# Moving sums and lo parts to VectorE, pooling the activations' sums in two, and loading the embedding at once in a fused encoder layer

## The chip, the cores and the metric

The kernel runs on one core of a Trainium2 chip. The metric is the device time of one execution in microseconds (us); lower is better. Engines are named as the profile has them: PE is TensorE's matmul and PEld its weight load, DVE is VectorE, ACT is ScalarE, POOL is GpSimd, SP is the engine that issues most DMAs.

## The reference

One layer of an encoder trunk, for a prompt of 1024 tokens and a sample of 64 (1088 columns here), in float32. In short:

```
xn = rmsnorm(x, norm_mix);  parts = xn @ w_in          # three mixers A, B, C
x  = x + concat(ya, yb, yc) @ w_out                     # output projection, 1536 -> 1024
h  = rmsnorm(x, norm_ffn)
g  = causal_conv3(h @ w_gate)                           # 1024 -> 3072
x  = x + (gelu(g) * (h @ w_up)) @ w_down                # gated MLP
x  = x + sigmoid(rmsnorm(x, norm_ple) @ ple_w_gate) * (p @ ple_w_proj)   # embedding p, 256 wide
y  = rmsnorm(x, norm_final)
```

The states of the mixers and convolutions are outputs too; the change doesn't touch them.

## The kernel before

Activations lie with features on the partitions and tokens along the free dimension, in three chunks of 384, 384 and 320 columns (`CH`). Float32 accuracy comes from split operands: `split` (line 182) writes a hi part by ScalarE (line 184, a copy rounded to fp32r) and a lo part `l = x - h` by a second engine (line 188), and each product is three matmuls, hi x hi, hi x lo and lo x hi (`mm3`, line 156). If no engine is given, the lo part alternates between VectorE and POOL (`alt`, line 180). For weights `unit_load` (line 115) has SP load 512 KB into one of two buffers `wr`, and `unit_split` (line 122) splits it, always with POOL, into a buffer `wh` and a buffer `wl`, of which wpool has three each; `wslots` names the pools in turn.

The program is traced in the order of the text, and a planner then fixes each engine's own order ahead of time, by priority in text order among what it expects to be ready, and places all semaphores. At run time each engine works through its list. A pool of tiles lies on a stack of bytes (or, with side="right", on one from the other end); a pool opened after others are closed takes their bytes.

The stages around the change, in order:
- Output projection in three passes of 512 rows of `w_out` (lines 1023, 1027 and 1086). In the last pass `add_proj` (line 997) loads four weight units first and goes chunk by chunk; `acc` (line 990) adds each result in PSUM to X (`L992`), and squares and their sums are made for the norm (`L208`, `L209`). Lanes are generators that `tick` (line 141) advances every six matmuls: `embedding` (line 1035) loads the nine blocks of p three ahead (`L1041`), turns them with PE (`L1051`) and splits them into pTh and pTl; `norm_rows` (line 1061) scales X in place once a chunk is complete (`L1067`), and after chunk 1 splits the left half of X into qh and ql (`lefts`).
- The embedding's projection (lines 1090 to 1099): two weight units, 24 results, copied to `po` by ScalarE (`L1098`) and written to DRAM.
- The two large products of the MLP run as quads, a Strassen-Winograd scheme: 2 x 2 blocks of weights (128 columns by 512 rows) times 2 x 2 blocks of X (512 rows by 544 columns, `HF`), with seven products instead of eight. The sums of X's blocks (t1, t2, t3, t4 and the plain b22) are made once, in two column parts of 224 and 320 (lines 1116 to 1128), in tiles of the pool rp. For each quad `quad_weights` (line 1140) loads two units, makes s1 to s4 by four POOL operations of 512 elements, and splits seven blocks. `quad` (line 1170) runs the products with three PSUM tiles qa, qb and qd in the order a11, s2, s1, a12, s3, s4, a22; the second four add onto what PSUM holds, so the copy `L1177` and the sums `L1179` to `L1189` have to be done in time.
- 12 pairs of quads, gate and up (lines 1212 to 1237), with the convolution on VectorE (`L1199`, `L1205`, `L1207`) between; results go to DRAM (`hidd`).
- Down projection, six groups (line 1291); norm (`rms`, line 1268); the gate of the embedding and the output (line 1345 on).

The bytes that a partition holds for the pools around the change: xnp (split activations of the last pass) 34,816; ept 26,624 (pTh and pTl 17,408, pt 3 x 1024, po 4 x 1536); wx 24,576; and on the same bytes, after all three are closed, rp with ten tiles of 8704 (87,040) and w2 with s12, s34, dh and dl (12,288).

Of the kernel before, what the change touches and what calls it, by code (L numbers as in the profile page):

```python
# [9 lines left out]
F32 = mybir.dt.float32  # L10
F32R = mybir.dt.float32r
# [16 lines left out]
BLK = [(b // 3, (b % 3) * 128, 128) for b in range(8)] + [(2, 256, 64)]  # L28
# [3 lines left out]
HF = 544  # L32
# [3 lines left out]
def f32(ap):  # L36
    return ap.bitcast(F32)
# [3 lines left out]
def trunk(ctx: ExitStack, tc: tile.TileContext, I, O):  # L41
    nc = tc.nc
    V, A, G, PE, SY = nc.vector, nc.scalar, nc.gpsimd, nc.tensor, nc.sync

    const = ctx.enter_context(tc.tile_pool(name="const", bufs=1))
    wpool = ctx.enter_context(tc.tile_pool(name="wpool", bufs=3))
# [17 lines left out]
    def sm_tile():  # L64
        return smps[0].tile([128, 512], F32, tag="sm", name="sm")
# [44 lines left out]
            pass  # L110


    wslots = {"pools": [wpool], "n": 0}

    def unit_load(ap):

        kt, cols = ap.shape[0] // 128, ap.shape[1]
        raw = wpool.tile([128, kt, cols], F32, tag="wr", name="wr", bufs=2)
        SY.dma_start(raw, ap.rearrange("(k p) n -> p k n", p=128))
        return raw  # L120

    def unit_split(raw):

        pool = wslots["pools"][wslots["n"] % len(wslots["pools"])]
        wslots["n"] += 1
        hi = pool.tile(list(raw.shape), F32R, tag="wh", name="wh")
        lo = pool.tile(list(raw.shape), F32R, tag="wl", name="wl")
        split(hi, lo, raw, G)
        return hi, lo

    def unit(ap):
        return unit_split(unit_load(ap))
# [4 lines left out]
    def lane(gen):  # L137
        lanes.append([gen, 0])
        return gen
# [40 lines left out]
    alt = [V, G]  # L180

    def split(h, l, x, eng=None):

        A.activation(h, x, AF.Copy)  # L184
        if eng is None:
            eng = alt[0]
            alt.reverse()
        eng.tensor_sub(l, x, f32(h))  # L188
# [35 lines left out]
    def tokens(name, b):  # L224
        lead = "a b t d -> (a b t) d" if name == "p" else "b t d -> (b t) d"
        if b < 8:
            return I[name + "_prompt"].rearrange(lead)[b * 128:(b + 1) * 128, :]
        return I[name + "_sample"].rearrange(lead)
# [78 lines left out]
    SY.dma_start(smw[:, :, 32:40], W[:, 4112:4120].rearrange("(k p) n -> p k n", p=128))  # L307
    finish(*[lane(xblock(b)) for b in range(3)])
    wq.append(unit_split(wraw))
    V.tensor_scalar(smh[:, :, 40:64], smw[:, :, 0:24], 0.0, None, op0=OP.mult)  # L310
    split(smh[:, :, 0:40], smh[:, :, 64:104], smw, V)
# [322 lines left out]
    for s in range(2):  # L634
        src = I["ssd_d"]
# [4 lines left out]
    for t, nm in ((dtb, "ssd_dt_bias"), (nea, "ssd_a_log")):  # L640
        src = I[nm]
# [389 lines left out]
    ept = est.enter_context(tc.tile_pool(name="ept", bufs=1, reuse_waits="tile"))  # L1031
# [2 lines left out]

    def embedding():

        pts = {}

        def pload(b):
            pts[b] = ept.tile([128, 256], F32, tag="pt", name="pt", bufs=3)  # L1040
            SY.dma_start(pts[b][:BLK[b][2], :], tokens("p", b))  # L1041

        for b in range(3):
            pload(b)
        yield 4
        for b, (c, off, L) in enumerate(BLK):
            pt = pts.pop(b)
            t0 = CH[c][0] + off
            ps = sm_tile()
            for k in range(2):  # L1050
                PE.transpose(ps[:, k * 128:k * 128 + L], pt[:L, k * 128:(k + 1) * 128], ident[:L, :L])  # L1051
            yield 1
            split(pTt[0][:, :, t0:t0 + L], pTt[1][:, :, t0:t0 + L],
                  ps.rearrange("p (k t) -> p k t", k=4)[:, 0:2, :L], V)
            if b + 3 < 9:
                pload(b + 3)
            yield 1

    lefts = []
# [18 lines left out]
    def spill(c, m):  # L1078
        t0, w = CH[c]
        if m % 2:  # L1080
            SY.dma_start(xspill[:, m - 1:m + 1, t0:t0 + w], XK[m // 4][:, m % 4 - 1:m % 4 + 1, t0:t0 + w])

    emb = lane(embedding())
    wslots["pools"], wslots["n"] = [wpool, wpool, wpool, wx], 0
    normed = []
    add_proj(WO[1024:1536], ys["c"], 4, lambda c: normed.append(lane(norm_rows(c))), spill)
# [19 lines left out]


    rst = ExitStack()
    rp = rst.enter_context(tc.tile_pool(name="rp", bufs=1, reuse_waits="tile"))
    w2 = rst.enter_context(tc.tile_pool(name="w2", bufs=1, reuse_waits="tile"))  # L1110

    def half(name):
        return tuple(rp.tile([128, 4, HF], F32R, name=name + n) for n in "hl")

    b22, t2, t1, t3, t4 = [half(n) for n in ("b22", "t2", "t1", "t3", "t4")]
    for a, n in ((0, 224), (224, 320)):
        s = slice(a, a + n)
        x11, x12 = XK[0][:, :, a:a + n], XK[0][:, :, HF + a:HF + a + n]
        x21, x22 = XK[1][:, :, a:a + n], XK[1][:, :, HF + a:HF + a + n]
        split(b22[0][:, :, s], b22[1][:, :, s], x22)  # L1120
        V.tensor_sub(x22, x22, x12)
        G.tensor_sub(x12, x12, x11)  # L1122
        V.tensor_add(x11, x22, x11)
        split(t2[0][:, :, s], t2[1][:, :, s], x11, V)
        split(t1[0][:, :, s], t1[1][:, :, s], x12, G)
        V.tensor_sub(x21, x21, x11)
        split(t3[0][:, :, s], t3[1][:, :, s], x22, V)
        split(t4[0][:, :, s], t4[1][:, :, s], x21, G)
    b11, b21 = [tuple(t[:, 4 * i:4 * i + 4, :] for t in lefts) for i in range(2)]
    xst2.close()  # L1130

# [8 lines left out]
    def quad_weights(ap):  # L1140

        raw0, raw1 = unit_load(ap[:, 0:128]), unit_load(ap[:, 128:256])
        a11, a12, a21, a22 = raw0[:, 0:4, :], raw0[:, 4:8, :], raw1[:, 0:4, :], raw1[:, 4:8, :]
        al = unit_split(raw0)
        s12 = w2.tile([128, 8, 128], F32, tag="s12", name="s12")
        s1, s2 = s12[:, 0:4, :], s12[:, 4:8, :]
        G.tensor_add(s1, a21, a22)
        G.tensor_sub(s2, s1, a11)
        be = unit_split(s12)
        s34 = w2.tile([128, 8, 128], F32, tag="s34", name="s34")  # L1150
        s3, s4 = s34[:, 0:4, :], s34[:, 4:8, :]
        G.tensor_sub(s3, a11, a21)
        G.tensor_sub(s4, a12, s2)
        ga = unit_split(s34)
        de = tuple(w2.tile([128, 4, 128], F32R, tag=n, name=n) for n in ("dh", "dl"))
        split(de[0], de[1], a22, G)
        part = lambda u, i: tuple(t[:, 4 * i:4 * i + 4, :] for t in u)
        return {"a11": part(al, 0), "a12": part(al, 1), "s1": part(be, 0), "s2": part(be, 1), "s3": part(ga, 0),
                "s4": part(ga, 1), "a22": de}
# [10 lines left out]
    def quad(ap, take11, o12, o21, o22):  # L1170

        w = quad_weights(ap)
        A_, B_, D_ = [qp.tile([128, 2, 512], F32, tag=n, name=n) for n in ("qa", "qb", "qd")]
        pa, pb, pd = [t[:, :, :HI] for t in (A_, B_, D_)]
        o12, o21, o22 = [t.rearrange("p (i n) -> p i n", i=2) for t in (o12, o21, o22)]
        prod(A_, w["a11"], b11, True)
        A.activation(o21, pa, AF.Copy)  # L1177
        prod(B_, w["s2"], t2, True)
        V.tensor_add(o12, o21, pb)  # L1179
        prod(D_, w["s1"], t1, True)  # L1180
        V.tensor_add(o22, o21, pd)
        prod(A_, w["a12"], b21, False)
        take11(pa)
        prod(B_, w["s3"], t3, False)
        V.tensor_add(o22, o22, pb)
        prod(D_, w["s4"], b22, False)
        V.tensor_add(o12, o12, pd)
        prod(B_, w["a22"], t4, False)
        V.tensor_add(o21, o21, pb)  # L1189
# [125 lines left out]
    src = I["norm_final"]  # L1315
# [90 lines left out]
```

## Time and profile before

| | us |
|---|---|
| median of 3 runs (1711.34 to 1718.62) | 1712.57 |
| the profiled execution | 1712.1 |
| its span in the trace | 1710.4 |
| PE busy in the span | 1616.9 (95%) |
| DVE busy | 945.4 (55%) |
| ACT busy | 698.7 (41%) |
| POOL busy | 696.3 (41%) |

The profile is one execution. Its page gives busy times, 40 slices of the span, the chain of work that ended last, and the costliest groups of instructions. "L188" is a line of the kernel; since `split` is a helper, all lo parts have line 188 and hi parts line 184, and the tile's name tells them apart. Matmuls are pipelined: two in a row overlap, so the time from one start to the next is the cost of one. In a timeline the bracket at a row's end gives how long its engine was idle before it, and who released it.

### The profile page before, as it was taken

The numbers are of one execution on the slowest core, as the hardware profiler recorded it, in microseconds if no ns is written. First come the engines' busy times: TensorE is split into PE (matmuls) and PEld (weight loads), VectorE is DVE, ScalarE is ACT, GpSimd is POOL, SyncE is SP. The second block draws the span as 40 slices with busy tenths as digits, with TensorE's granted clock in tenths as the row PEclk, the third lists the DMA queues.
The fourth block names the chain that finished last, engine by engine and source line by source line (L and its number), as shares of the span: only waits on it lengthen the run. The fifth ranks groups of instructions, "written<-read, shape, count | busy, mean of one in ns | idle before, by whom it ended". The sixth has DMA issues, their size and how long they took to land.

```text
span 1710.4 us, 27185 instructions
## 1 busy us (share of the span) xinstructions
PE 1616.9 (95%) x10990; PEld 1557.8 (91%) x10990; DVE 945.4 (55%) x1565; ACT 698.7 (41%) x1041; POOL 696.3 (41%) x589
## 2 busy tenths in 40 slices
PE   6999999999999899876999999999998999999997
PEld 6888889878999798876999999999998999999996
DVE  5588783785545832755455555555554333336944
ACT  5588773676623312343333333333333211103526
POOL 3232332122221423345766666666664523221410
PEclk8999999999999899987999999999999999999998
DMA  7322114012652113230222222222227532210223
GB/s 229 83 80 60 43 58 104 17 38 75 196 167 68 51 50 102 96 128 25 76 77 76 76 76 76 77 76 76 76 76 283 181 102 80 75 50 13 65 72 122
DMA packets 169225, 151.81 MB, mean 89 GB/s; under 512 B 11330, under 2 KB 157644, under 8 KB 169100
## 3 DMA queue, kind: packets, MB, share of 16 engines
q1 hardware_dynamic: 159740, 145.62, 27.6%
q10 hardware_dynamic: 9360, 4.46, 0.9%
q8 instruction: 86, 1.41, 0.3%
q14 instruction: 39, 0.32, 0.1%
HBM read 111.26 MB, written 38.79 MB: 88 GB/s over the span
## 4 chain that ended last, share of the span: by engine, by line
PE 53%; DVE 4%; POOL 3%; issue 2%; ACT 2%; DMA 2%; SPq 0%; POOLq 0%; DVEq 0%; ACTq 0%
PE mm L163 24%; PE qb L1166 13%; PE qd L1166 8%; PE qa L1166 8%; POOL wl L188 1%; DVE nr_x L1281 1%; DVE nr_t L218 1%; DMA wr<-in_ple_w_proj_dram 0%; ACT yo L1329 0%; ACT wh L184 0%; POOL X L1122 0%; DVE u L1179 0%; POOL dl L188 0%; POOL ql L188 0%; DVE nr_t L209 0%
## 5 line engine op out<-in xcount | busy, mean ns | idle before, releaser
L188 POOL TENSOR_TENSOR wl<-wr,wh 128x1024 fp32r<-128x1024 f32 x102 | 247.2, 2425 | 420.6 <-ACT wh L184 411.9
L163 PE MATMUL mm<-dh,wl 128*128 128x384 f32 (+1 forms) x768 | 252.0, 328 | 2.7 <-POOL wl L188 2.7
L163 PE MATMUL mm<-dh,wh 128*128 128x384 f32 (+1 forms) x768 | 252.0, 328 | 2.0 <-ACT wh L184 2.0
L163 PE MATMUL mm<-dl,wh 128*128 128x384 f32 (+1 forms) x768 | 251.6, 328 | 1.1 <-DVE dl L188 0.9
L184 ACT ACTIVATE wh<-wr 128x1024 fp32r<-128x1024 f32 x102 | 107.7, 1057 | 349.4 <-PE mm L163 209.7
L163 PE MATMUL mm<-h,wh 128*128 128x384 f32 (+1 forms) x528 | 179.6, 341 | 16.1 <-ACT h L184 8.7
L163 PE MATMUL mm<-l,wh 128*128 128x384 f32 (+1 forms) x528 | 177.8, 337 | 6.2 <-DVE l L188 6.2
L163 PE MATMUL mm<-h,wl 128*128 128x384 f32 (+1 forms) x528 | 180.8, 342 | 0.0
L992 DVE TENSOR_TENSOR Xq<-Xq,mm 128x384 f32<-128x384 f32 (+1 forms) x144 | 75.9, 530 | 158.1 <-PE mm L163 157.1
L163 PEld LDWEIGHTS mm<-dh,wl 128*128 128x128 f32 x768 | 144.8, 189 | 3.1 <-POOL wl L188 3.1
L163 PEld LDWEIGHTS mm<-dh,wh 128*128 128x128 f32 x768 | 144.8, 188 | 2.6 <-ACT wh L184 2.2
L163 PEld LDWEIGHTS mm<-dl,wh 128*128 128x128 f32 x768 | 144.8, 189 | 2.1 <-DVE dl L188 1.1
L163 PE MATMUL mm<-ql,wh 128*128 128x384 f32 (+1 forms) x432 | 144.2, 334 | 0.2 <-POOL ql L188 0.2
L163 PE MATMUL mm<-qh,wh 128*128 128x384 f32 (+1 forms) x432 | 142.1, 329 | 0.0
L163 PE MATMUL mm<-qh,wl 128*128 128x384 f32 (+1 forms) x432 | 141.8, 328 | 0.0
L188 POOL TENSOR_TENSOR wl<-s,wh 128x1024 fp32r<-128x1024 f32 x48 | 118.1, 2461 | 15.1 <-ACT wh L184 15.1
L163 PEld LDWEIGHTS mm<-h,wh 128*128 128x128 f32 x528 | 101.5, 193 | 21.8 <-ACT h L184 9.7
L163 PEld LDWEIGHTS mm<-l,wh 128*128 128x128 f32 x528 | 102.1, 193 | 9.4 <-DVE l L188 7.0
L1166 PE MATMUL qa<-ql,wh 128*128 128x272 f32 x384 | 110.6, 288 | 0.0
L1166 PE MATMUL qa<-qh,wh 128*128 128x272 f32 x384 | 110.5, 288 | 0.0
L1166 PE MATMUL qa<-qh,wl 128*128 128x272 f32 x384 | 110.3, 287 | 0.0
L163 PEld LDWEIGHTS mm<-h,wl 128*128 128x128 f32 x528 | 102.1, 193 | 2.5 <-issue 0.6
(400 smaller groups left out, 4320.7 us busy)
## 6 DMA issues: line engine op xcount, KB each, us to landing
wr<-in_w_in_dram SPq DMA_DIRECT2D x32, 512.0 KB
hidd<-ft SPq DMA_DIRECT2D x24, 544.0 KB
wr<-in_ffn_w_gate_dram SPq DMA_DIRECT2D x24, 512.0 KB
wr<-in_ffn_w_up_dram SPq DMA_DIRECT2D x24, 512.0 KB
wr<-in_ffn_w_down_dram SPq DMA_DIRECT2D x24, 512.0 KB
st<-hidd SPq DMA_DIRECT2D x12, 768.0 KB
wr<-in_w_out_dram SPq DMA_DIRECT2D x12, 512.0 KB
s_cb<-cumd SPq DMA_DIRECT2D x18, 256.0 KB
```

The lines of the kernel that those rows point to most:

```text
L163: PE.matmul(out, w, x, start=(k == 0), stop=(k == n - 1))
L184: A.activation(h, x, AF.Copy)
L188: eng.tensor_sub(l, x, f32(h))
L218: V.reciprocal(tot, tot)
L992: V.tensor_add(xv(c, m), xv(c, m), ps[:, :w])
L1166: PE.matmul(ps[:, i, :HI], wt[:, k, :], xt[:, k, HI * i:HI * i + HI], start=new and n == 0, stop=n == 11, skip_group_check=True)
L1281: V.scalar_tensor_tensor(x, xv(c, f), gain[:, f:f + 1], tot, op0=OP.mult, op1=OP.mult)
```

## The change

- From the lane of the embedding on, `alt` holds VectorE alone and `wslots["eng"]` is VectorE: all lo parts behind this place, of weights and of activations, are VectorE's. The weight units of the output projection's last pass are among them.
- The four sums of each quad's weights and the lo part of a22 are VectorE's too.
- The sums of the activations are made in another order, all by VectorE: first x12 - x11 (t1), then x22 - t1 (t2, in x12's place), then t2 - x11 (t3) and x21 - t2 (t4); b22 is split late. t1 and t2 are in a pool rp1 of their own, t3, b22 and t4 in rp2.
- The embedding's nine blocks are loaded by two DMAs at the start of the lane, into pt8 (8192 bytes a partition) and pt1 (1024), in place of the three buffers pt; the lane's first wait is twelve steps, not four.

```diff
-    wslots = {"pools": [wpool], "n": 0}
+    wslots = {"pools": [wpool], "n": 0, "eng": G}
...
-        split(hi, lo, raw, G)
+        split(hi, lo, raw, wslots["eng"])
...
-        for b in range(3):
-            pload(b)
-        yield 4
+        pt8 = ept.tile([128, 8, 256], F32, name="pt8")
+        pt1 = ept.tile([64, 256], F32, name="pt1")
+        src = tokens("p", 0)
+        SY.dma_start(pt8, bass.AP(tensor=src.tensor, offset=src.offset, ap=[[256, 128], [128 * 256, 8], [1, 256]]))
+        SY.dma_start(pt1, tokens("p", 8))
+        yield 12
...
-            if b + 3 < 9:
-                pload(b + 3)
...
     emb = lane(embedding())
+    alt[:] = [V]
+    wslots["eng"] = V
...
-    rp = rst.enter_context(tc.tile_pool(name="rp", bufs=1, reuse_waits="tile"))
+    rp1 = rst.enter_context(tc.tile_pool(name="rp1", bufs=1, reuse_waits="tile"))
+    def half(name, pool):
+        return tuple(pool.tile([128, 4, HF], F32R, name=name + n) for n in "hl")
+    t1, t2 = [half(n, rp1) for n in ("t1", "t2")]
+    rp2 = rst.enter_context(tc.tile_pool(name="rp2", bufs=1, reuse_waits="tile"))
+    t3, b22, t4 = [half(n, rp2) for n in ("t3", "b22", "t4")]
     w2 = rst.enter_context(tc.tile_pool(name="w2", bufs=1, reuse_waits="tile"))
-    b22, t2, t1, t3, t4 = [half(n) for n in ("b22", "t2", "t1", "t3", "t4")]
...
+        V.tensor_sub(x12, x12, x11)
+        split(t1[0][:, :, s], t1[1][:, :, s], x12)
+        V.tensor_sub(x12, x22, x12)
+        split(t2[0][:, :, s], t2[1][:, :, s], x12)
+        V.tensor_sub(x11, x12, x11)
+        V.tensor_sub(x21, x21, x12)
+        split(t3[0][:, :, s], t3[1][:, :, s], x11)
         split(b22[0][:, :, s], b22[1][:, :, s], x22)
-        V.tensor_sub(x22, x22, x12)
-        G.tensor_sub(x12, x12, x11)
-        V.tensor_add(x11, x22, x11)
-        split(t2[0][:, :, s], t2[1][:, :, s], x11, V)
-        split(t1[0][:, :, s], t1[1][:, :, s], x12, G)
-        V.tensor_sub(x21, x21, x11)
-        split(t3[0][:, :, s], t3[1][:, :, s], x22, V)
-        split(t4[0][:, :, s], t4[1][:, :, s], x21, G)
+        split(t4[0][:, :, s], t4[1][:, :, s], x21)
...
-        G.tensor_add(s1, a21, a22)
-        G.tensor_sub(s2, s1, a11)
+        V.tensor_add(s1, a21, a22)
+        V.tensor_sub(s2, s1, a11)
...
-        G.tensor_sub(s3, a11, a21)
-        G.tensor_sub(s4, a12, s2)
+        V.tensor_sub(s3, a11, a21)
+        V.tensor_sub(s4, a12, s2)
...
-        split(de[0], de[1], a22, G)
+        split(de[0], de[1], a22)
```

## Rows read from the trace of the kernel before

**Rows 1.** The page, busy us (share of the span) and instructions:

```profile
PE 1616.9 (95%) x10990; PEld 1557.8 (91%) x10990; DVE 945.4 (55%) x1565; ACT 698.7 (41%) x1041; POOL 696.3 (41%) x589
```

**Rows 2.** Table by stretch: length, busy PE, PEld, DVE, ACT, POOL; granted clock, DMA, GB/s:

```profile
655.00:695.00 40.00, 33.14 (x197) 31.87 (x196) 14.02 (x29) 11.33 (x22) 18.05 (x10) 1.00 0.43 137
695.00:740.00 45.00, 37.80 (x213) 36.41 (x212) 38.60 (x50) 17.27 (x29) 20.00 (x8) 0.92 0.26 88
...
760.00:793.00 33.00, 11.52 (x69) 10.67 (x68) 19.10 (x13) 11.25 (x12) 20.73 (x11) 0.64 0.02 8
793.00:1298.00 505.00, 498.29 (x3960) 496.26 (x3959) 258.57 (x274) 166.12 (x180) 340.25 (x299) 1.00 0.24 77
1298.00:1310.00 12.00, 7.03 (x26) 6.46 (x27) 7.61 (x5) 4.26 (x4) 9.91 (x4) 0.72 0.97 341
1310.00:1560.00 250.00, 250.00 (x1516) 250.00 (x1515) 88.65 (x142) 46.85 (x43) 77.31 (x29) 1.00 0.34 109
1560.00:1620.00 60.00, 58.05 (x350) 56.58 (x349) 52.78 (x82) 32.09 (x58) 21.02 (x16) 1.00 0.11 31
```

**Rows 3.** What PE waited for, 480 to 800: us, times, longest:

```profile
PE qd L1166 <- ACT t1h L184: 18.5, 1, 18.5
PE mm L163 <- DVE X L992: 7.2, 2, 3.8
...
PE sm L1051 <- DVE pTl L188: 3.7, 2, 2.2
PE sm L1051 <- DMA pt<-in_p_prompt_dram: 3.2, 1, 3.2
```

**Rows 4.** What PE waited for, 800 to 1711:

```profile
PE qb L1166 <- DVE u L1179: 6.7, 8, 0.9
PE mm L163 <- POOL wl L188: 2.7, 1, 2.7
```

**Rows 5.** Timeline of PE, start and us: first matmul of two products:

```profile
758.94 0.32 PE L1166 MATMUL qa<-qh,wh 128*128 128x272 f32 x1
...
792.70 0.29 PE L1166 MATMUL qa<-qh,wh 128*128 128x272 f32 x1
```

**Rows 6.** Chain that ended last, 780 to 870: start, us, what:

```profile
792.86 3.02 PE qa L1166 x24
...
859.85 3.29 PE qb L1166 x24
```

**Rows 7.** Timelines of DVE and ACT around the activations' sums:

```profile
743.72 3.79 DVE L1067 SCALAR_TENSOR_TENSOR X<-X,cols,nr_t 128x320 f32<-128x320 f32 x8
762.69 1.09 DVE L1121 TENSOR_TENSOR X<-X,X 128x896 f32<-128x896 f32 x1 [15.18 <-POOL b22l L188]
...
759.52 2.11 ACT L184 ACTIVATE b22h<-X 128x896 fp32r<-128x896 f32 x2
...
788.95 0.61 ACT L1177 ACTIVATE fraw<-qa 128x544 f32<-128x544 f32 x1
```

**Rows 8.** Timelines of DVE and POOL at 724; DVE's group by form:

```profile
724.00 6.33 DVE L1067 SCALAR_TENSOR_TENSOR X<-X,cols,nr_t 128x384 f32<-128x384 f32 x2
...
724.78 5.14 POOL L188 TENSOR_TENSOR ql<-X,qh 128x2176 fp32r<-128x2176 f32 x1
...
L1067 DVE SCALAR_TENSOR_TENSOR X<-X,cols,nr_t 128x384 f32<-128x384 f32 x16 | 18.0, 1170 | 0.0
```

**Rows 9.** The page, costliest groups: busy, mean ns | idle before:

```profile
L188 POOL TENSOR_TENSOR wl<-wr,wh 128x1024 fp32r<-128x1024 f32 x102 | 247.2, 2425 | 420.6 <-ACT wh L184 411.9
...
L184 ACT ACTIVATE wh<-wr 128x1024 fp32r<-128x1024 f32 x102 | 107.7, 1057 | 349.4 <-PE mm L163 209.7
```

**Rows 10.** Timeline of DVE: lo parts of 896 and 1280 elements:

```profile
772.04 1.08 DVE L188 TENSOR_TENSOR t2l<-X,t2h 128x896 fp32r<-128x896 f32 x1
...
784.86 1.48 DVE L188 TENSOR_TENSOR t2l<-X,t2h 128x1280 fp32r<-128x1280 f32 x1
```

**Rows 11.** L1199 on DVE: ns min/median/max, first and last start:

```profile
L1199 DVE SCALAR_TENSOR_TENSOR ft<-fraw,cols,ft x48: 1343/1548/2553, 804.1 to 1282.6; 128x1088 f32<-128x1088 f32 x48
```

More of the change, by code (lines that the diff above doesn't have):

```diff
@@ L1035, in embedding @@
     def embedding():
[L1037 to L1041, printed above, removed]
-        for b in range(3):
-            pload(b)
-        yield 4
+        pt8 = ept.tile([128, 8, 256], F32, name="pt8")
[4 more added lines that the diff above has]
+        yield 12
         for b, (c, off, L) in enumerate(BLK):
-            pt = pts.pop(b)
+            pt = pt8[:, b, :] if b < 8 else pt1
             t0 = CH[c][0] + off
@@ L1108, in trunk @@
     rst = ExitStack()
-    rp = rst.enter_context(tc.tile_pool(name="rp", bufs=1, reuse_waits="tile"))
+    rp1 = rst.enter_context(tc.tile_pool(name="rp1", bufs=1, reuse_waits="tile"))
[4 more added lines that the diff above has]
+    t3, b22, t4 = [half(n, rp2) for n in ("t3", "b22", "t4")]
     w2 = rst.enter_context(tc.tile_pool(name="w2", bufs=1, reuse_waits="tile"))
-    def half(name):
-        return tuple(rp.tile([128, 4, HF], F32R, name=name + n) for n in "hl")
-    b22, t2, t1, t3, t4 = [half(n) for n in ("b22", "t2", "t1", "t3", "t4")]
     for a, n in ((0, 224), (224, 320)):
```

## Prediction, made before the changed kernel was run

> **What bounds the kernel now.** The page's busy line comes first: TensorE (PE) is busy 1617 of 1710 us, VectorE (DVE) 945, GpSimd (POOL) 696 [rows 1]. So a faster engine elsewhere is worth only the PE idle time that it removes. Next the table by stretch [rows 2], cut where the page's PE slices sink: PE is idle for 6.9 us in the last pass of the output projection (655 to 695), 7.2 in the end of it and the start of the embedding's projection (695 to 740), 21.5 around the start of the MLP (760 to 793), 6.7 in the 505 us of the MLP's first part, 5.0 at the start of the down projection (1298 to 1310), 2.0 in the norm ahead of the last projection (1560 to 1620). The list of what PE waited for [rows 3, 4] names the late engine of each, and the timelines [rows 5, 7, 8] show why. What lies ahead of 655 and behind 1620 is the same in both kernels and costs the same.
>
> The trace spans 1710.4 us, the profiled execution took 1712.1, and the median of the three runs is 1712.57. I sum against 1712.1.
>
> **Sums of the activations (lines 1108 to 1130), 760 to 793.** The first quad product starts at 758.94, straight behind the embedding's projection, and the fourth at 792.70 [rows 5]. A product takes 3.01 us [rows 6], so without waits the fourth would start at 758.94 + 3 x 3.01 = 767.97: 24.7 us are lost, 18.5 of them in one wait for t1h [rows 3]. The granted clock of the stretch is 0.64 [rows 2], so the products behind the wait run in part at 1.2 instead of 2.4 GHz; that is inside the 24.7. Why is t1 late? The normalisation of X's last chunk is over at 743.72 + 3.79 = 747.5, and VectorE then idles 15.2 us, up to the first sum; that waits for b22, which ScalarE writes from 759.52 on, when the last copy of the embedding's projection is done [rows 7]. The first half of b22h reads only chunk 1 of X, normalised long before. The pool rp lies on the bytes of xnp, ept and wx, and its first tile comes only when all three are done with. I take from this that the order on each engine, which is planned ahead, puts a pool's first write behind the last use of every pool under it.
>
> The change makes t1 and t2 a pool of their own: 4 x 8704 = 34,816 bytes a partition, just what xnp held, and xnp is free when the output projection ends. The first sum touches only X. t1 and t2 need eight instructions of VectorE, four of 896 and four of 1280 elements: 4 x 1.08 + 4 x 1.48 = 10.2 us [rows 10], in a stretch in which it idles; half of that needs only chunks 0 and 1 and can go earlier. So the wait of 18.5 us goes.
>
> What is late next: t3, b22 and t4 (rp2) stay on ept and wx, and the weights' sums join them. By the tile sizes ept grows from 26,624 to 32,768 bytes (pt8 and pt1), so xnp, ept and wx now end at 92,160 bytes, past the 87,040 of rp1 and rp2: w2 (s12, s34, dh, dl) begins on wx's last 5120 bytes, where it lay clear before. The first quad's sums, made long ahead until now, then come behind the embedding's last matmul. From there: two sums of 512 elements at some 0.68 (estimate: the line through 896 and 1280 elements [rows 10]), the hi part at 1.06 [rows 9], the lo part at 1.21 (same line) make 3.6 us, against the 3.0 of the first product: 1 us late. The first copy out of PSUM (L1177, at 788.95 now [rows 7]) goes into a tile on X's bytes, so it comes behind the last reader of X: lo parts of t3, b22 and t4 3 x (1.08 + 1.48), one of weights 1.21 and four sums 2.7 are 11.6 us, plus 0.61 for the copy, against 9.0 + 1 when the fourth product wants it: 2 to 3 us late. So 4 to 5 of the 24.7 stay. Gain taken: **20**; ends: 24.7 (all of it hidden) and 14 (VectorE's queue in a worse order).
>
> **Lo parts and sums on VectorE, 695 to 740.** POOL's 2.43 us for 1024 elements [rows 9] become some 1.21. VectorE is busy 38.6 of 45 us here [rows 2], but not all of it is its own work: two instructions of L1067 took 6.33 us while POOL worked 5.14 at ql [rows 8]. At the 0.47 that a piece of 320 elements takes [rows 7] the two, of 384, would need 1.1. The 16 of this shape took 1.17 on average [rows 8], so some 9 us were lost in all. PE's 7.2 us are two waits for L992, queued behind these [rows 3]. With POOL silent the 9 us go; one ql (2.44, by the same line) and a lo part (1.21) come, and the first quads' other sums and lo parts leave for the stretch above. VectorE then has 33 us of work in 38: enough, but tight. Taken: **5** of the 7.2; ends: 9 (with the slow clock after the waits, 0.92 in the mean [rows 2]) and 0.
>
> **Embedding loaded at once, 655 to 695.** Nine loads of 128 KB become two, issued where the first three were. The 3.2 us wait for pt goes [rows 3]: six loads no longer queue behind weights on SP. The transposes begin twelve steps into the pass, not four, some 8 us later, past ScalarE's wait for the weights of the embedding's projection, behind which pTh, hence pTl and PE, stood (3.7 us [rows 3]). In return the nine pTl meet the norm of chunk 0 on VectorE. No row shows a 1 MB load beside the weights' loads; I bound its harm by 1 us. Taken: **5**; ends: 6.9 and 2.
>
> **The MLP's first part, 793 to 1298.** PE's 6.7 us are eight waits for L1179 [rows 4]; with the product behind each (3.29 instead of 3.01 [rows 6]) some 8.5 are lost. VectorE is in the convolution then (L1199: 1.34 to 2.55 us for one shape [rows 11]). The change adds to VectorE in each quad three lo parts of 1024 and five operations of 512 elements: 3 x 1.21 + 5 x 0.68 = 7.0 us, 14.1 in a pair of quads. Its 258.6 of 505 us [rows 2] are 22 in a pair's 43; with 14.1 that is 36 of 42, even if no row gets shorter. From the gate quad's last o12 to the product that needs the up quad's L1179 five products pass, 15 us; at 36 of 42 the work in them is 12.9, with the convolution in this half perhaps 14. The waits go if the order follows due times. Taken: **8**; ends: 8.5 and 3.
>
> **Down projection and last norm.** At the down projection's start PE waits 2.7 us for POOL's wl [rows 4]; wl gets shorter, but two dl now stand ahead of it on VectorE: **2** (0 to 6). From 1310 to 1560 VectorE has 88.7 us of 250 and PE never waits [rows 2]; some 40 us more stay hidden. From 1560 to 1620 it is busy 52.8 of 60 us [rows 2]: 12 lo parts of some 0.5 and four of 1.21 add 11, and rows lengthened by POOL may lose as much: **0** (+2 to -6).
>
> A rule of the Trainium skill speaks against the change: Perfetto Trace Analysis, section Optimizing Scalar/DVE Operations, says that with VectorE saturated it may pay to give work away, even to GpSimd, but adds that the two share a read port, so that it might not help. By the first half the sum would be that of rival 3; by the second, with which the pair in [rows 8] agrees, it stays.
>
> **Sum:** 20 + 5 + 5 + 8 + 2 + 0 = 40; 1712.1 - 40 = **1672**. With the upper ends, 57: 1655; with the lower ones, 18: 1694.
>
> **Rivals.**
> 1. The wait only changes its cause: rp1 doesn't come early, or the first quad's sums, on wx's bytes, are queued last. If t1 and t2 start at 759, they need their 10.2 us and the hi parts between, some 14 (estimate), 11 more than the first product covers; with the 4 to 5 above 9 us are gained instead of 20: 1683. If also the quad's sums stand behind all six lo parts (7.7 us), 1691. For it: the overlap of w2 and wx. Against: rp1 fills xnp exactly.
> 2. It doesn't do what it says: in the new order other operations come late, and only some 10 us remain: 1702.
> 3. VectorE is full: the long rows of 695 to 740 and 1560 to 1620 are its own work. Then 11 us on top of 52.8 in 60 cost 10, the 5 of the first stretch are lost and 3 paid: 1712 - 35 + 13 = 1690. Against it: [rows 8].
> 4. Slower: in the MLP, VectorE's queue has the lo part of the up quad's first weights behind the convolution of the gate quad. PE would wait at the first product of each up quad for four L1199 (5.4) and the lo part, 6.6 us, 6 after some slack: 72 in 12 pairs, 1712 - 32 + 72 = 1752. It decides from 32 / 12 = 2.7 us a pair on. Against it: with POOL's slower lo parts there is one wait for wl, and it lies behind the MLP's first part [rows 4].
>
> **Chances.** Forecast (1655 to 1694) 0.60; rival 1 0.12; rival 2 0.08; rival 3 0.10; rival 4 0.10. Within 0.5% (8.6 us, about what a measurement of this kernel tells from no change), 1704 to 1721, lie much of rival 2 and the light end of rival 4: 0.07. Faster: 0.83; slower: 0.10. The range goes from the forecast's lower end, 1655, over rivals 1 and 3 to 1701; rival 4 and half of rival 2 are left out.
>
> **What would show it.** In the changed profile: t1 and t2 written while the embedding's projection runs, PE's wait for t1h gone; waits of 1 to 3 us at the first quad's second and fourth product, for be (from s12) and L1177; no wait for pt; no L1067 far above 0.6; no waits for L1179, and 42.1 us from pair to pair; VectorE near 36 of 42 in the MLP. I am wrong if PE waits in every quad for a lo part by VectorE, if t1 still comes behind the embedding's last copy, or if the last norm grows by several us.

## The result, and the profile after

The changed kernel takes 1672.72 us in the median of four runs (1672.37 to 1674.28), against 1715.43 for the kernel before (1711.34 to 1718.62): a ratio of 0.9754, 95% interval 0.9727 to 0.9781. Forecast were 1672 and a range of 1655 to 1701. By the medians that is 42.7 us. By profiled executions it is 1712.1 against 1674.28, their spans 1710.4 and 1672.6: 37.8 us, where the sum said 40. The total is right, but not all of its terms are.

The busy line of the page, which answers to [rows 1]; lines that stood behind the changed places are one to five lower now (L1067 is L1062, L1166 is L1165, L1179 is L1178, L1199 is L1198):

```profile
PE 1611.8 (96%) x10990; PEld 1556.1 (93%) x10990; DVE 1064.8 (64%) x1824; ACT 701.7 (42%) x1041; POOL 205.7 (12%) x330
```

The table by stretch of the changed kernel, columns as in [rows 2]: the last pass of the output projection, its end, the first quad's start, the rest of the MLP's first part, and 250 us of the down projection:

```profile
655.00:695.00 40.00, 40.00 (x237) 39.57 (x236) 25.83 (x41) 12.53 (x21) 0.00 (x0) 1.00 0.36 116
682.00:727.00 45.00, 41.81 (x256) 40.20 (x255) 39.27 (x65) 19.88 (x37) 0.00 (x0) 1.00 0.24 86
746.00:770.00 24.00, 16.52 (x97) 15.58 (x97) 20.02 (x22) 10.75 (x13) 1.98 (x4) 0.72 0.22 68
770.00:1263.00 493.00, 493.00 (x3937) 493.00 (x3937) 335.04 (x453) 168.69 (x178) 26.15 (x116) 1.00 0.25 80
...
1273.00:1523.00 250.00, 250.00 (x1513) 250.00 (x1513) 119.25 (x169) 46.58 (x44) 0.00 (x0) 1.00 0.34 110
```

PE never idles in the last pass and in the MLP behind its start. What is left in these stretches lies at the end of the output projection (3.2 us) and at the first quad (7.5); a little more is left at the start of the down projection, in the waits for wh and dl (2.5 and 0.8). The list of PE's waits, 480 to the end, names them; it answers to [rows 3, 4]:

```profile
PE mm L163 <- DVE X L992: 5.5, 3, 2.3
PE qb L1165 <- ACT wh L184: 4.7, 1, 4.7
PE mm L163 <- ACT wh L184: 2.5, 1, 2.5
...
PE qb L1165 <- DVE wl L188: 2.2, 1, 2.2
...
PE mm L163 <- DVE dl L188: 0.8, 1, 0.8
PE qa L1165 <- ACT fraw L1176: 0.6, 1, 0.6
```

No pt, no pTl, no t1h, no sum behind a quad's second product. The new waits, for wh and wl, are at the first quad. The timelines there (all engines in one, cut), from the first lo part of t1:

```profile
726.25 1.08 DVE L188 TENSOR_TENSOR t1l<-X,t1h 128x896 fp32r<-128x896 f32 x1
...
745.48 1.48 DVE L188 TENSOR_TENSOR t2l<-X,t2h 128x1280 fp32r<-128x1280 f32 x1
746.15 0.39 PE L1165 MATMUL qa<-qh,wh 128*128 128x272 f32 x1
748.28 0.69 DVE L1146 TENSOR_TENSOR s<-wr 128x512 f32<-128x512 f32 x1
750.69 1.08 DVE L188 TENSOR_TENSOR t3l<-X,t3h 128x896 fp32r<-128x896 f32 x1
751.86 1.26 ACT L184 ACTIVATE t4h<-X 128x1280 fp32r<-128x1280 f32 x1
753.02 1.04 ACT L184 ACTIVATE wh<-s 128x1024 fp32r<-128x1024 f32 x1
754.12 0.59 PE L1165 MATMUL qb<-t2h,wh 128*128 128x272 f32 x1 [4.68 <-ACT wh L184]
756.50 1.48 DVE L188 TENSOR_TENSOR t4l<-X,t4h 128x1280 fp32r<-128x1280 f32 x1
757.90 1.21 DVE L188 TENSOR_TENSOR wl<-s,wh 128x1024 fp32r<-128x1024 f32 x1
759.17 0.59 PE L1165 MATMUL qb<-t2h,wl 128*128 128x272 f32 x1 [2.17 <-DVE wl L188]
```

The quad's sums s12 start at 748.28, behind the embedding's projection, and then both engines take the splits of t3, b22 and t4 first: wh comes behind six copies of ScalarE, wl behind six lo parts of VectorE.

To place gains I cut every profiled execution at the same five events. Zero is one sum into X (L992, the 39th from the last, near 639 us); then the first matmul of the first quad's first product, the first of its fifth, the last matmul of the MLP's first part, the first transposes (L1328, after L1327) of the last projection:

| kernel | ratio (95%) | zero | to 1st product | to 5th | to last | to transposes |
|---|---|---|---|---|---|---|
| before | 1 | 638.4 | 120.5 | 36.8 | 501.9 | 368.3 |
| changed | 0.9754 (0.9727 to 0.9781) | 639.7 | 106.4 | 23.9 | 493.0 | 365.5 |
| w2_clear | 0.9705 (0.9680 to 0.9729) | 637.2 | 108.8 | 13.9 | 493.1 | 365.6 |
| old_load | 0.9702 (0.9672 to 0.9731) | 635.5 | 107.0 | 13.9 | 493.1 | 365.4 |
| one_pool | 0.9778 (0.9754 to 0.9801) | 638.1 | 106.3 | 28.3 | 493.0 | 365.5 |
| two_pools_alone | 0.9862 (0.9833 to 0.9891) | 641.7 | 122.9 | 14.0 | 500.8 | 368.4 |
| mlp_pool | 0.9825 (0.9807 to 0.9843) | 637.6 | 107.5 | 24.2 | 503.4 | 366.1 |
| ql_pool | 0.9753 (0.9734 to 0.9772) | 637.0 | 105.5 | 23.6 | 493.0 | 365.4 |
| down_pool | 0.9815 (0.9795 to 0.9835) | 637.2 | 106.4 | 22.6 | 493.0 | 374.0 |
| load_alone | 0.9954 (0.9938 to 0.9971) | 637.6 | 118.8 | 37.1 | 500.8 | 369.1 |
| wl_pool | 0.9767 (0.9750 to 0.9783) | 639.2 | 108.5 | 22.9 | 493.0 | 365.0 |
| wl_old | 0.9729 (0.9712 to 0.9745) | 636.8 | 112.3 | 13.9 | 493.1 | 366.2 |
| wl_ql_pool | 0.9767 (0.9750 to 0.9783) | 639.6 | 108.6 | 23.1 | 493.0 | 365.2 |
| old_load_l4 | 0.9684 (0.9666 to 0.9702) | 639.7 | 103.7 | 16.0 | 493.0 | 366.1 |

So the 37.8 us are -1.3 ahead of zero, 14.1 up to the first product, 12.9 in the first quad, 8.9 in the rest of the MLP's first part, 2.8 from there to the transposes and 0.5 at the end.

### The profile page after: what moved, and what is told of

Same layout as the page of the kernel before. It is cut to its first block, busy times and chain, and to the rows that moved or that the text cites. A ratio compares the mean times of both kernels' runs of the same rounds, so it can differ in the third digit from the quotient of the medians.

```text
span 1672.6 us, 27037 instructions
## 1 busy us (share of the span) xinstructions
PE 1611.8 (96%) x10990; PEld 1556.1 (93%) x10990; DVE 1064.8 (64%) x1824; ACT 701.7 (42%) x1041; POOL 205.7 (12%) x330
## 4 chain that ended last, share of the span: by engine, by line
PE 61%; DVE 3%; ACT 1%; issue 0%; DVEq 0%; ACTq 0%
PE mm L163 30%; PE qb L1165 13%; PE qd L1165 9%; PE qa L1165 8%; DVE nr_t L218 0%; PE sm L1327 0%; DVE ql L188 0%; ACT yo L1328 0%; DVE X L1062 0%; DVE l L188 0%; DVE yc L986 0%; DVE dl L188 0%; PE sm L216 0%; ACT yo L1338 0%; DVE X L992 0%
## 5 line engine op out<-in xcount | busy, mean ns | idle before, releaser
L163 PE MATMUL mm<-h,wh 128*128 128x384 f32 (+1 forms) x528 | 178.4, 339 | 12.9 <-ACT h L184 8.5
L992 DVE TENSOR_TENSOR Xq<-Xq,mm 128x384 f32<-128x384 f32 (+1 forms) x144 | 76.0, 530 | 113.6 <-PE mm L163 113.0
L188 POOL TENSOR_TENSOR wl<-wr,wh 128x1024 fp32r<-128x1024 f32 x40 | 95.8, 2397 | 170.1 <-ACT wh L184 162.6
L184 ACT ACTIVATE wh<-s 128x1024 fp32r<-128x1024 f32 x48 | 51.0, 1061 | 155.2 <-PE qd L1165 55.0
L1165 PE MATMUL qa<-qh,wh 128*128 128x272 f32 x384 | 110.9, 289 | 0.6 <-ACT fraw L1176 0.6
L1165 PE MATMUL qa<-ql,wh 128*128 128x272 f32 x384 | 110.8, 288 | 0.0
L1165 PE MATMUL qa<-qh,wl 128*128 128x272 f32 x384 | 110.4, 288 | 0.0
```

Source lines behind the costliest of these rows:

```text
L163: PE.matmul(out, w, x, start=(k == 0), stop=(k == n - 1))
L992: V.tensor_add(xv(c, m), xv(c, m), ps[:, :w])
L1165: PE.matmul(ps[:, i, :HI], wt[:, k, :], xt[:, k, HI * i:HI * i + HI], start=new and n == 0, stop=n == 11, skip_group_check=True)
```

## Experiments: the first quad

**w2_clear** keeps w2 off wx's bytes.

```diff
+    ptst = ExitStack()
+    ptp = ptst.enter_context(tc.tile_pool(name="ptp", bufs=1, reuse_waits="tile"))
...
-        pt8 = ept.tile([128, 8, 256], F32, name="pt8")
-        pt1 = ept.tile([64, 256], F32, name="pt1")
+        pt8 = ptp.tile([128, 8, 256], F32, name="pt8")
+        pt1 = ptp.tile([64, 256], F32, name="pt1")
...
     finish(emb)
+    ptst.close()
+    pop = est.enter_context(tc.tile_pool(name="pop", bufs=4, reuse_waits="tile"))
...
-                po = ept.tile([128, w], F32, tag="po", name="po", bufs=4)
+                po = pop.tile([128, w], F32, tag="po", name="po")
```

> The changed kernel with one thing moved: pt8 and pt1 lie in a pool of their own above wx, and the four buffers po take those bytes once the transposes are done. xnp, ept, wx and this pool end at 86,016 bytes, below the 87,040 of rp1 and rp2, so w2 no longer starts on bytes of wx. Theory A (the overlap of w2 with wx is what held back the first quad's sums): s12 is written before the embedding's projection ends, PE's waits for wh (4.7 us) and wl (2.2 us) ahead of the second product go, and the slow clock behind them. In the changed kernel the fifth product of the first quad starts 24.1 us after the first, where four products of 3.01 make 12.0; with a wait of about 1 us left for the first copy out of PSUM I expect 13 to 15 us, so 9 to 11 us less, minus up to 3 us for four sums and two lo parts more on VectorE while it normalises the last chunk: 1665, range 1661 to 1668. Rival B (the sums come late because VectorE's queue has the lo parts of the activations first, wherever w2 lies): s12 still behind 748, no change, 1672.

1665.37 us (1663.76 to 1666.79). From first to fifth product 13.9 us instead of 23.9; four products make 12.0. The first of the 24 groups of sums starts at 677.3, not 748 (its line with ns min/median/max, first and last start), and of PE's waits between 740 and 800 one is left:

```profile
L1150 DVE TENSOR_TENSOR s<-wr x24: 678/691/694, 677.3 to 1216.5; 128x512 f32<-128x512 f32 x24
...
PE qa L1169 <- ACT fraw L1180: 1.5, 1, 1.5
```

Theory A holds, in size too: 10 us of the first quad hung on the 5120 bytes that w2 shared with wx; old_load, which frees them in another way, shows the same 13.9. The profiled execution of w2_clear pays 2.4 of them back ahead of the first product.

**old_load** undoes the loading alone, by which ept shrinks and w2 is clear of wx as well.

```diff
-        pt8 = ept.tile([128, 8, 256], F32, name="pt8")
-        pt1 = ept.tile([64, 256], F32, name="pt1")
...
-        yield 12
+        for b in range(3):
+            pload(b)
+        yield 4
...
+            if b + 3 < 9:
+                pload(b + 3)
```

> The changed kernel with the embedding loaded as before: three buffers pt, nine loads, the lane's first wait four steps. This undoes the third part of the change alone. Theory A: the stretch of the output projection's last pass loses what the change gave it, 5 to 8.5 us (waits for pt and pTl of 3.2 and 3.7 come back), and since ept shrinks to 26,624 bytes w2 is clear of wx, and the first quad's waits of 4.7 and 2.2 us go, 8 to 11 us gained: between 1666 and 1673, 1670 taken. Rival B (w2's place is not the cause of the first quad's waits): only the loss, 1678 to 1681. Rival C (loading at once is worth nothing beside the silent POOL): the gain alone, 1663.

1664.79 us (1660.48 to 1669.08), between the expectations of A and C. The first quad is as in w2_clear, and the stretch ahead of it takes 107.0 us against 106.4 in the changed kernel and 108.8 in w2_clear, which has w2 clear too and the new loading kept. So beside a silent POOL the loading at once gains nothing that these runs show, and no wait for pt or pTl comes back. As the change has it, the new loading costs: its bytes push w2 onto wx.

**one_pool** makes t1 to t4 and b22 one pool again, the new order kept.

```diff
-    rp2 = rst.enter_context(tc.tile_pool(name="rp2", bufs=1, reuse_waits="tile"))
-    t3, b22, t4 = [half(n, rp2) for n in ("t3", "b22", "t4")]
+    t3, b22, t4 = [half(n, rp1) for n in ("t3", "b22", "t4")]
```

> The changed kernel with t1, t2, t3, b22 and t4 in one pool again, in the changed order of the sums. Theory A (a pool's first write comes behind the last use of every pool under it): the first sum waits until the last copy of the embedding's projection, near 746, and t1 and t2 start then. VectorE needs 10.2 us for their two column parts and the four hi parts come between, so the second and third product come some 8 to 12 us later than in the changed kernel: 1682, range 1679 to 1687. Rival B (tiles are waited for one by one, and the new order alone brought t1 early): no change, 1672.

1677.77 us (1676.97 to 1678.8), 5 more, a little below A's range. The intervals of the two ratios overlap, so the case rests on the waits. VectorE idles 10.4 us ahead of its first instruction for the quads, and PE waits for t1 and t2:

```profile
744.61 0.69 DVE L1145 TENSOR_TENSOR s<-wr 128x512 f32<-128x512 f32 x1 [10.37 <-PE mm L163]
...
PE qd L1164 <- ACT t1h L184: 2.9, 1, 2.9
PE qd L1164 <- DVE t1l L188: 2.4, 1, 2.4
...
PE qb L1164 <- DVE t2l L188: 2.1, 1, 2.1
```

The pool is what brings t1 early (A). It costs less than expected because in this order the quad's sums come ahead of t1: PE has no wait for the quad's wh or wl here, so the 4.7 and 2.2 of the changed kernel are not paid on top.

**two_pools_alone** is the kernel before with the pools and the order of the activations' sums alone, all by VectorE (that part of the diff; its five `split` with a V more).

> The kernel before with the two pools and the new order of the activations' sums alone, all of these by VectorE; POOL keeps the weights' lo parts and sums and half of the lo parts, and the embedding is loaded as before, so w2 is clear of wx. Theory A (what the prediction's term of 20 us rests on): the waits for t1h (18.5) and t1l (2.4) go, and some 20 us of 24.7 are gained: 20 below the kernel before. Rival B (while POOL works, VectorE's rows in the stretch 695 to 740 are long, and t1 and t2 find no room there): they are written behind the embedding's projection, and 10 us are gained.

1692.35 us (1691.34 to 1694.07), 24.3 below the kernel before in the same runs. The first quad falls from 36.8 to 14.0: 22.8 of the 24.7 that the prediction counted as lost. Up to the first product it takes 2.4 us more, with 7.8 us of waits for L992 (7.2 before, [rows 3]). A holds, and the edit alone is worth more there than inside the change, since w2 stays clear.

## Experiments: POOL beside VectorE

**mlp_pool** gives the quads' lo parts and all four sums (s1 to s4) back to POOL; behind the quads `wslots["eng"]` is VectorE again.

```diff
+    wslots["eng"] = G
...
-        V.tensor_add(s1, a21, a22)
+        G.tensor_add(s1, a21, a22)
...
-        split(de[0], de[1], a22)
+        split(de[0], de[1], a22, G)
```

> The changed kernel with the quads' weights as before: the four sums, the lo parts and that of a22 by POOL; VectorE again from the down projection on. Theory A (POOL's work lengthens VectorE's rows, and that, not VectorE's own share, made the eight waits of 0.83 us): the rows of the convolution, 1335/1346/1353 ns (min/median/max) in the changed kernel, go back to about 1343/1548/2553 as before, the waits for the sum behind the gate quad's second product return, and some 8 us with them; the first quad may gain 0 to 3 where POOL works beside VectorE: 1679, range 1677 to 1682. Rival B (the order of VectorE's queue made the waits): VectorE has 14 us a pair less to do, no wait returns, 1670 to 1673.

1684.3 us (1683.17 to 1687.54), 11.6 more; 10.4 of it in the rest of the MLP's first part. Nine waits are back (7.9 us), although VectorE has less to do there: 261.0 busy of 503 us against 335.0 of 493.

```profile
769.00:1272.00 503.00, 494.85 (x3931) 492.80 (x3931) 261.01 (x276) 165.56 (x179) 334.51 (x300) 1.00 0.25 78
...
PE qb L1166 <- DVE u L1179: 7.9, 9, 1.2
...
L1199 DVE SCALAR_TENSOR_TENSOR ft<-fraw,cols,ft x48: 1343/1548/2494, 777.8 to 1257.7; 128x1088 f32<-128x1088 f32 x48
```

In the changed kernel this row is

```profile
L1198 DVE SCALAR_TENSOR_TENSOR ft<-fraw,cols,ft x48: 1335/1346/1353, 778.5 to 1246.9; 128x1088 f32<-128x1088 f32 x48
```

What stands directly ahead of the late sum is, in mlp_pool and then in the changed kernel (the same pair of quads; cut, VectorE alone):

```profile
870.94 1.26 DVE L1207 SCALAR_TENSOR_TENSOR ft<-sx,cols,ft 128x2 f32<-128x2 f32 x1
872.12 1.34 DVE L1205 TENSOR_SCALAR ft<-sx,cols,cols 128x2 f32<-128x2 f32 x1
873.50 2.61 DVE L1207 SCALAR_TENSOR_TENSOR ft<-sx,cols,ft 128x2 f32<-128x2 f32 x2
876.03 0.71 DVE L1179 TENSOR_TENSOR u<-u,qb 128x544 f32<-128x544 f32 x1
...
869.30 0.21 DVE L1206 SCALAR_TENSOR_TENSOR ft<-sx,cols,ft 128x2 f32<-128x2 f32 x1
869.43 0.28 DVE L1204 TENSOR_SCALAR ft<-sx,cols,cols 128x2 f32<-128x2 f32 x1
869.62 0.71 DVE L1178 TENSOR_TENSOR u<-u,qb 128x544 f32<-128x544 f32 x1
```

Four rows of two elements take 5.2 us there; at the lengths of the changed kernel they would take 0.9. Two such rows come ahead of the sum in mlp_pool alone, but that order is worth only 0.4 us at 0.21 each. A holds: rows beside POOL are longer, and that made the waits; the size is above its range. B falls, since with 14 us a pair less to do VectorE is late.

**ql_pool** moves `alt[:] = [V]` behind `finish(emb)`; **wl_pool** leaves `wslots["eng"]` with POOL up to the quads; **wl_ql_pool** does both.

> The changed kernel with the lo parts of activations alternating between VectorE and POOL to the end of the embedding's lane, so that one of the two ql is POOL's again. Theory A (contention): two pieces of the normalisation beside ql take about 6 us instead of 1.1, PE's waits for X, 3.2 us in the changed kernel, grow to 7 or 8, and the slow clock behind them is longer: 4 to 6 us more, 1677. Rival B (VectorE's own work bounds this stretch): one ql of 2.33 us leaves VectorE, and the time falls by 1 to 3 us, 1670.

> The changed kernel with the weights' lo parts left to POOL from the output projection's last pass to the end of the embedding's projection (2.43 us each instead of 1.21), VectorE from the quads on. The stretch from the last pass to the first quad product gained 14.1 us, and neither the loading at once (its removal left 0.6 us of difference in this stretch) nor ql's engine (none) made that. Theory A (the weights' lo parts on POOL made it, by long rows on VectorE and by holding the weights' buffers and SP's queue longer): 8 to 14 us come back, 1682, range 1679 to 1687. Rival B (no part alone does, each goes round the same waits): up to 3 us, 1672 to 1676.

> The changed kernel with the weights' lo parts by POOL up to the quads, and one ql by POOL too, the loading at once kept. Alone these cost 2.1 and -0.9 us of the stretch. Theory A (two POOL instructions at a time are needed to lengthen VectorE's rows enough; the kernel before with the new loading alone still took 118.8 us for the stretch, against 106.4 in the changed kernel): 8 to 12 us come back there, 1682. Rival B (they add up): 1 to 3 us, 1675.

1672.32 (1670.17 to 1675.11), 1676.16 (1674.19 to 1677.39) and 1676.06 us (1674.68 to 1677.27). All three theories A fall in their size: the stretch up to the first product becomes 0.9 us shorter, 2.1 and 2.2 longer. wl_pool and wl_ql_pool come out as their rivals B said, ql_pool as neither. The lengthening itself is there. In ql_pool POOL's ql and VectorE's lie side by side, and VectorE's takes twice its 2.42 of the changed kernel (POOL's 5.17 is its usual pace, 5.14 in [rows 8]):

```profile
711.99 5.17 POOL L188 TENSOR_TENSOR ql<-X,qh 128x2176 fp32r<-128x2176 f32 x1 [79.92 <-ACT qh L184]
...
714.47 4.97 DVE L188 TENSOR_TENSOR ql<-X,qh 128x2176 fp32r<-128x2176 f32 x1
```

The Trainium skill, Perfetto Trace Analysis, section Optimizing Scalar/DVE Operations, says that work moved between these two engines might not help, since they share a read port; VectorE's 4.97 us beside POOL's ql agrees, and mlp_pool, where such work goes back to POOL, loses 11.6 us. But this long row cost nothing: four of the last five sums into X came ahead of it, and PE waits 2.1 us for the fifth, where in the changed kernel it waits 2.1 and 1.1 us behind the two ql. In the kernel before, five POOL instructions lay beside the normalisation of chunk 1 (715 to 730: two lo parts, two sums, ql), and the pieces of L1067 took 1.17 us on average [rows 8]; in wl_ql_pool, where POOL has no work beside them but the start of ql, the same 16 take 0.61. So what counts is which POOL instruction lies beside which row, not POOL's share. Four of those five belong to the quads' weights, and no run built from the changed kernel puts them back at this place: what they cost there is not measured.

**wl_old** is wl_pool and old_load together.

> The changed kernel with two things undone together: the old loading of the embedding, and POOL for the weights' lo parts up to the quads. Alone, the first cost 0.6 us and the second 2.1 us of the 14.1 that the stretch from the output projection's last pass to the first quad product had gained. Theory A (loads and lo parts go round the same wait: nine small loads on SP's queue behind weights whose buffers POOL's slower lo parts hold): together they cost far more than 2.7, some 8 us, PE's waits for pt and pTl come back; w2 is clear of wx, which gives 8 to 10 at the first quad: 1672, range 1669 to 1676. Rival B (the two add up): some 3 us in the stretch, 1667.

1669.5 us (1667.6 to 1672.74), inside A's range. The stretch is 5.9 us longer than in the changed kernel, where the two alone made 0.6 and 2.1, and of the two waits of the kernel before that A expected one is back, for pTl but not for pt:

```profile
PE sm L1051 <- DVE pTl L188: 3.4, 2, 2.0
```

Loads and lo parts go round the same wait, so their gains don't add.

**load_alone** is the kernel before with the loading of w2_clear alone.

> The kernel before with the new loading of the embedding alone: two loads, first wait twelve steps; pt8 and pt1 in a pool of their own whose bytes po takes over, so that w2 stays clear of wx. Theory A (the prediction's term: the loads behind weights on SP's queue and the late pTl cost 5 to 6.9 us): the waits for pt and pTl go, 5 to 7 us less than the kernel before, the first quad product near 753. Rival B (with all else changed the old loading cost nothing, as the run with the old loading shows no wait for pt; so POOL's slow lo parts, which hold up the weights' buffers and with them SP's queue, are the cause, and the two loads only go round it): also 5 to 7 us less here, since the loads no longer stand behind weights, but none in the changed kernel. Rival C: the transposes meet the norm on VectorE and lose as much, 0 to 2 us less.

1707.47 us (1702.55 to 1712.09, ten runs), 7.4 below the kernel before (interval 5.0 to 10.6 by the ratio). The waits for pt and pTl go, but PE waits 3.3 us for nr_t ahead of a transpose, and 8.4 for L992 (7.2 before). In the profiled execution the stretch gains only 1.8 us, and the span 3.3. The times speak for A and B, the profile for C; but the profiled execution of the kernel before lies 2.8 us below the median of these runs and that of load_alone 1.4 above its own, so the pair can't show 4.2 of the 7.4 us. A and B differ only in the changed kernel, where old_load speaks for B; where the gain lies stays open.

**down_pool** sets `wslots["eng"] = G` and `alt[:] = [V, G]` ahead of the down projection.

> The changed kernel with the down projection as before: weights' lo parts by POOL, those of the activations alternating. Theory A (the start of the down projection and the last norm gained 2.8 us together because POOL is silent): 2 to 4 us more, 1675.5. Rival B (the prediction's 0 for the norm, and the start as good on either engine): 1672 to 1673.5.

1682.15 us (1678.99 to 1685.1). From the MLP's last matmul to the transposes 374.0 us: 8.5 more than in the changed kernel, and 5.7 more than in the kernel before. Two waits of PE carry it:

```profile
PE mm L163 <- DVE dl L188: 4.7, 1, 4.7
PE sm L216 <- DVE nr_t L209: 3.3, 2, 2.9
```

The first comes from a dl of VectorE that lies beside one of POOL:

```profile
1260.60 4.38 POOL L188 TENSOR_TENSOR dl<-st,dh 128x1536 fp32r<-128x1536 f32 x1 [2.12 <-ACT dh L184]
1261.62 4.98 DVE L188 TENSOR_TENSOR dl<-st,dh 128x1536 fp32r<-128x1536 f32 x1
```

In the changed kernel two such rows of VectorE take 3.42 us. A holds in sign, but the loss is over twice what it expected and more than the change gained there, so how the 2.8 us of the change came about is not shown.

## Experiment: a faster version

**old_load_l4** is old_load with four steps of the lane ahead of each split of X's left half.

```diff
             for i in range(2):
+                yield 4
                 split(h[:, 4 * i:4 * i + 4, :], l[:, 4 * i:4 * i + 4, :], XK[i][:, :, 0:HF])
```

> The changed kernel with the embedding loaded as before, and four steps of the lane ahead of each of the two splits of X's left half, so that the sums into X of the last chunk come ahead of the second ql on VectorE. In the run with the old loading alone PE waits 2.1 and 1.2 us for these sums behind two ql of 2.4 us. Theory A: both waits shrink below 1 us, the first quad product starts 2 to 4 us earlier and nothing else is late: 1661, range 1658 to 1664. Rival B: VectorE has the same work ahead of t1 and t2 in any order, the wait moves to the second or third product of the first quad: 1664 to 1667.

1663.2 us (1658.86 to 1664.36), the lowest ratio, but not clear of old_load by the intervals. Both theories have a part: the stretch up to the first product is 3.4 us shorter than in old_load, PE's waits for L992 there, 3.3 us, are gone, and the first quad takes 2.1 us more, with a wait of 2.2 instead of 1.5 for the first copy. old_load, w2_clear and this one are 7.4 to 9.5 us faster than the changed kernel in the median, this one alone clear of it by the intervals.

## Why the prediction was right, and where it was not

- **Sums of the activations: taken 20 (14 to 24.7), measured 12.9, below the lower end.** t1 and t2 came as said: their first lo parts at 726.25 and 730.44, the last over at 747, and PE never waits for them. The step that failed is what is late next. I had s12's hi and lo part come 1 us late, ahead of the lo parts of t3, b22 and t4; they come behind them, 4.7 and 2.2 us of waits and a slow clock (0.72 in the stretch). The cause was named (w2 on wx's bytes) and the order was priced under rival 1 (7.7 us), but given 0.12 with the rest of that rival. With w2 clear the term is 22.8 to 22.9. The copy, expected 2 to 3 us late at the fourth product, was 0.6.
- **Up to the first product: taken 5 + 5, measured 14.1.** PE's 14.1 us of idle time in the two stretches are 3.2 now, and the slow clock behind the waits (0.92) is gone: 10.9 us of idle time, and for the clock the other 3.2 (an estimate, by difference), which the sum had only in its upper end. The long rows went as said: the 16 pieces of L1067 take 9.0 us now, 18.0 before. But the causes were wrongly parted. The loading at once got a term of 5; taken out of the changed kernel it costs 0.6. Nor is it ql alone. Put back one at a time, the loads, the weights' lo parts of the last pass and one ql cost 2.1 us at most, loads and lo parts together 5.9; the rest of the 14.1 is not assigned to a part by any run.
- **The MLP's first part: taken 8, measured 8.9.** Right, by the cause too. VectorE's share was wrong: 28.6 of 42.1 us (335.0 / 493), not 36. The added work was right (wl 1.23 and sums 0.69 measured, 1.21 and 0.68 in the sum). What lay there before got shorter by some 7 us a pair, which the prediction did not count ("even if no row gets shorter"). Rival 4 needed a lo part behind the convolution; no wait for one is in the list.
- **Down projection and norm: taken 2 + 0, measured 2.8.** VectorE in the 250 us has 119.3 us, 30.6 more and all hidden, where some 40 were forecast.
- **Ahead of 655: taken 0, measured -1.3.** All these kernels run the same instructions in the same order up to the last pass, and zero still lies between 635.5 and 641.7. The program doesn't explain this spread, and it is as large as several of the terms.

That the total came out so close is luck: 7.1 too much in the first term met 4.1 too little in the second and 0.9, 0.8 and 0.5 in the last three, less the 1.3. The lower ends, as the prediction gives them, add up to 13 (14 + 0 + 2 + 3 + 0 - 6), not 18, so its forecast should have reached to 1699; nothing else in it hangs on that. Of the six signs under "what would show it" four held as written; the waits at the first quad and VectorE's 36 did not.

## What to carry to other kernels

A tile that grows moves every pool stacked above it: before merging loads into a bigger tile, look up which later pool then begins on whose bytes, and what its first write has to wait for. When an engine's rows differ in length for one shape, look at what the other engine does beside them before counting the first as full: work may be taken over at a profit where the busy shares speak against it. Parts that go round the same wait are worth their gain once, so cost them together and test them in pairs.

## What the runs showed of the hardware

In these groups, whether a VectorE row grows beside POOL goes with what it reads. Groups by form in the MLP's first part (busy us, mean ns), first of the kernel before:

```profile
L1207 DVE SCALAR_TENSOR_TENSOR ft<-sx,cols,ft 128x2 f32<-128x2 f32 x48 | 39.9, 831 | 0.8
L1235 DVE TENSOR_TENSOR ft<-ft,u 128x1088 f32<-128x1088 f32 x11 | 25.4, 2309 | 1.1
...
L1185 DVE TENSOR_TENSOR fraw<-fraw,qb 128x544 f32<-128x544 f32 x12 | 8.7, 722 | 63.5 <-PE qb L1166 63.5
```

then of the changed kernel:

```profile
L1234 DVE TENSOR_TENSOR ft<-ft,u 128x1088 f32<-128x1088 f32 x11 | 14.1, 1284 | 0.0
L1206 DVE SCALAR_TENSOR_TENSOR ft<-sx,cols,ft 128x2 f32<-128x2 f32 x48 | 10.3, 214 | 0.0
...
L1184 DVE TENSOR_TENSOR fraw<-fraw,qb 128x544 f32<-128x544 f32 x12 | 8.7, 723 | 9.8 <-PE qb L1165 9.8
```

Rows of two elements fell from 831 to 214 ns and the product with u from 2309 to 1284, while the sums that read a PSUM tile (qb) kept their 722, although 11 of these 12 lie beside POOL's rows in the kernel before. ql_pool fits this: the sums into X that lie beside POOL's ql there read PSUM and keep their length.

The rows don't slow each other down in proportion; the one that comes second seems to stand still until the first is over. VectorE's ql in ql_pool ends 2.3 us behind POOL's (719.44 and 717.16) and takes 2.42 alone; the dl in down_pool ends 1.6 us behind POOL's, and takes some 1.7 alone. In the kernel before it is POOL's sum that comes second:

```profile
732.43 2.44 DVE L188 TENSOR_TENSOR ql<-X,qh 128x2176 fp32r<-128x2176 f32 x1
732.66 3.36 POOL L1152 TENSOR_TENSOR s<-wr 128x512 f32<-128x512 f32 x1
735.98 1.30 POOL L1153 TENSOR_TENSOR s<-wr,s 128x512 f32<-128x512 f32 x1
```

VectorE's ql keeps its 2.44, and POOL's sum takes 3.36 us where the next takes 1.30. So even a row of two elements can cost as long as what is left of POOL's row. I had counted on shorter rows in the normalisation; that 48 rows of two elements cost 40 us, I had not seen.
